# A Fourier layer in which a product, a norm's scaling and the reading of spectra are given other places in the order of work

## The chip, the cores and the metric

The kernel runs on one core of one Trainium2 chip. The core has five engines that the text names: TensorE (PE in the views, with PEld for its weight loads), VectorE (DVE), ScalarE (ACT), GpSimd (POOL) and SyncE (SP, which here only issues DMAs). Each engine works through its own instructions in the order in which the program lists them, and instructions wait on semaphores for work of other engines. The metric is the time of one execution of the whole program on the device, in microseconds (us), smaller is better.

## The reference, cut to what matters

Two inputs of 2048 and 512 positions by 1024 channels pass through two layers and a last norm. The first layer is windowed attention and isn't touched by the change. The second is Fourier mixing with a gate:

```python
def fourier_layer(x, g, w_gate, w_out):
    h = rmsnorm(x, g)
    hg = h.reshape(b, s, N_FGROUPS, FGROUP_CH)
    f = jnp.fft.fftn(hg, axes=(1, 3), norm="ortho").real
    gate = h @ w_gate
    return x + (f * jax.nn.silu(gate)) @ w_out
...
return rmsnorm(x, final_norm)
```

So each output row needs the transform over all positions (f), a product with the gate (silu of a projection), a projection back (w_out), the sum with the row of x, and a norm of that row with its scale.

## The kernel before, in words

The attention layer takes most of the span and is left out here. The Fourier layer transforms first over the channels and then over the positions. The positions are split by their remainder modulo 16: a short transform across the remainders gives spectra G[0] to G[8], and a 128 x 128 transform finishes each of them and gives 128 output rows (for k1 = 0 and 8) or two tiles of 128 rows (k1 and 16 - k1). The short input is treated likewise, with remainders modulo 4 (names with s0, s1, s2 instead of p0 to p8).

**A position.** `position(name, ...)` finishes one spectrum. Its loads are the gate's rows (`s2...`, 128 x 1024 each, from DRAM) and a table. For each half of the columns `halves_of` splits the spectrum into a high and a low part (`g..`, a cast on ACT, L1310, and a subtraction on DVE, L1311). PE multiplies them with the table into two PSUM banks (`A..`, `B..`); ACT copies A into `u..` (L1339, L1342), and DVE forms sums and differences with B (L1343 to L1346). At the end each tile u is multiplied by its gate's rows on DVE (L1348, 128 x 1024).

**A finish.** For the positions s0 to s2, p0, p8, p4 and p2, `split_T` transposes u on PE (`tru`) and splits it (`tTu`), and `finish(uT, r)` multiplies by the output weights. It loads 128 rows of x (`x2_r`, L1363), runs 24 matmuls of 512 columns into each of two PSUM tiles (`fo<r>_0`, `fo<r>_1`), adds them to x2 on DVE (L1374), and calls `normed`: a square with a sum on ACT (L969), the inverse root on DVE and POOL (`invf`, L88, L89), a scaling of 128 x 1024 on DVE (L1358) and the store by SP (L1359). `step` runs the positions of one spectrum, then finishes the tiles of the spectrum ahead of it.

**An Outs stage.** For p6, p1, p7, p3 and p5 the class `Outs` does the projection with fewer matmuls: `operands()` transposes the tiles (`tr6` and so on, 16 transposes on PE) and forms sums, differences and splits of them on ACT and DVE (`tT`, `F`, `S`; L1398, L1399, L1408, L1415, L942, L944), and `products` runs groups of 12 matmuls with weights and sums of weights (`Wo`, `Zo`, `Xo`; `fT`, `fN` are sums of weights that come back from DRAM, L1487), between which the hooks start the next position. `residual` and `normed` are the same as above (added by L1439).

**Rings.** The gate's rows and the x2 rows share one ring of four buffers of 128 x 1024 (tag "x"): a load into it waits until the tile that had the buffer is no longer needed. The PSUM tiles `fo`, `Wo`, `Zo`, `Xo`, and in the gates `W`, `Z`, `X`, share a ring of three banks (tag "acc"). The spectra G[7], G[3] and G[5] don't fit and go to DRAM (`god`, stored by ACT, L1637); `reads(k1)` brings each back as two tiles `go..` of 128 x 1024 (L1651).

**The gates.** `gates(pr, hooks)` makes the gate's rows of four tiles of positions with the same trick of shared products: groups of matmuls into W, Z and X, sums on DVE (the one of interest is `c22 += W`, L1142), then a tanh on ACT, a product on DVE (L1108) and a store. The hooks run other work between the groups; in the last call hook 3 holds the position s1 (`position(*one)`, tiles us1_0 and us1_1) and hook 5 its transposes.

The order of the instructions on each engine is settled when the program is built: a scheduler takes them from the code's order, moves independent ones past each other, and keeps what `after(ins, anchor)` asks for (ins is put behind anchor on the same engine, with no other effect).

Of the kernel before, what the change touches and what calls it, by code (L numbers as in the profile page):

```python
# [14 lines left out]
ALU = mybir.AluOpType  # L15
# [27 lines left out]
def encoder(  # L43
# [876 lines left out]
    def fourier_phase(tail):  # L920
        with ExitStack() as es:
# [15 lines left out]
            def zt(name):  # L937
                return right([P, D], F32, name)
# [134 lines left out]
                        ACT.activation(out, v[:, 1], AF.Copy, scale=scale)  # L1073
                        last_z[0] = DVE.scalar_tensor_tensor(out, v[:, 0], scale, out, ALU.mult, ALU.add)

            last_z = [None]

            def prod(out, a, b, ks, first):

# [14 lines left out]
            def gates(pr, hooks):  # L1094

                n, A, S = pr.n, pr.A, pr.S
                W = psum2.tile([P, 512], F32, tag="acc", name=f"W{n}")
                Z = psum2.tile([P, 512], F32, tag="acc", name=f"Z{n}")
                X = psum2.tile([P, 512], F32, tag="acc", name=f"X{n}")

                def x_step(k):
                    prod(X, A[0, 1], b21[4 * n : 4 * n + 4], (k,), True)
                    more()

                def silu(c, i, half):
                    th = main.tile([P, 512], F32, tag="xr", bufs=3, name=f"gt{pr.ts[i]}_{half}")
                    ACT.activation(th, c, AF.Tanh, scale=0.5)
                    DVE.scalar_tensor_tensor(th, th, 1.0, c, ALU.add, ALU.mult)  # L1108
                    t = pr.ts[i]
                    dst, t0 = (s2d[0], t) if t < SEQ // P else (s2d[1], t - SEQ // P)  # L1110
                    POOL.dma_start(dst[t0 * P : (t0 + 1) * P, half * 512 : half * 512 + 512], th)

                def hook(i):
                    for h in hooks.get(i, ()):
                        h()

                four = range(4)
                c = xtile([P, 2, 512], F32, f"c{n}")
                c11, c22 = c[:, 0], c[:, 1]
                prod(W, A[0, 0], wg["B11"], four, True)  # L1120
                ACT.copy(c11, W)
                hook(0)
                x_step(0)
                if pr is pairs[-1]:

                    more()
                    more()
                prod(Z, S[1], wg["T1"], four, True)
                ACT.copy(c22, Z)
                hook(1)  # L1130
                prod(W, S[2], wg["T2"], four, False)
                c12 = fp.tile([P, 512], F32, tag="c12", bufs=1, name=f"c12_{n}")
                ACT.copy(c12, W)
                hook(2)
                x_step(1)
                prod(Z, S[4], wg["B22"], four, False)
                DVE.tensor_tensor(c12, c12, Z, ALU.add)
                silu(c12, 0, 1)
                hook(3)
                x_step(2)  # L1140
                prod(W, S[3], wg["T3"], four, False)
                DVE.tensor_tensor(c22, c22, W, ALU.add)  # L1142
                silu(c22, 1, 1)
                hook(4)
                x_step(3)
                DVE.tensor_tensor(c11, c11, X, ALU.add)
                silu(c11, 0, 0)
                if pr is not pairs[-1]:
                    hook(5)
                prod(W, A[1, 1], wg["N4"], (0, 1), False)  # L1150
                if pr is pairs[-1]:
                    hook(5)
                prod(W, A[1, 1], wg["N4"], (2, 3), False)
                silu(W, 1, 0)
                hook(6)
# [156 lines left out]
                        out.append(t)  # L1312
                return out

            def position(name, tab, gr, gs, tiles, loads=None, parts=None, between=None):

                s2s, tb = loads or position_loads(name, tab, tiles)
                cs, sn, ns = [(tb[:, 2 * i], tb[:, 2 * i + 1]) for i in range(3)]
                bp = bank(f"B{name}")
                us = [zt(f"u{name}_{i}") for i in range(len(tiles))]  # L1320
                for hf in range(2):
                    ts = parts[hf] if parts else halves_of(name, gr, gs, hf)
                    if hf and between:
                        between()

                    def acc(out, tabs, c0, n):
                        for i, (w, t) in enumerate(zip(tabs, ts)):
                            v = [
                                t[:, part].rearrange("p (g c) -> p g c", g=2)[:, :, c0 : c0 + n]
                                for part in range(2)  # L1330
                            ]
                            matmul3(out, w, v, i == 0, i == len(ts) - 1)

                    a = bank(f"A{name}_{hf}")[:, :260].rearrange("p (g c) -> p g c", g=2)
                    acc(a, (cs, ns), 0, 130)
                    b = bp[:, hf * 256 : hf * 256 + 256].rearrange("p (g c) -> p g c", g=2)
                    acc(b, (sn, cs), P, P)
                    uv = [u.rearrange("p (g c) -> p g c", g=4)[:, 2 * hf : 2 * hf + 2] for u in us]
                    ACT.copy(uv[0][:, :, 0 : P + 1], a[:, :, 0 : P + 1])  # L1339
                    re, im = uv[0][:, :, 1:P], b[:, :, 1:P]  # L1340
                    for v in uv[1:]:
                        ACT.copy(v[:, :, 0 : P + 1 : P], a[:, :, 0 : P + 1 : P])  # L1342
                        DVE.tensor_tensor(v[:, :, 1:P], re, im, ALU.add)  # L1343
                        DVE.tensor_tensor(v[:, :, P + 1 : 256], re, im, ALU.subtract)
                    DVE.tensor_tensor(uv[0][:, :, P + 1 : 256], re, im, ALU.add)
                    DVE.tensor_tensor(re, re, im, ALU.subtract)  # L1346
                for u, s2 in zip(us, s2s):
                    DVE.tensor_tensor(u, u, s2, ALU.mult)  # L1348
                return list(zip(us, tiles))

            def out_rows(r):
                dst, off = (y_prompt, 0) if r[0] < SEQ else (y_sample, SEQ)
                return rows(dst, (r[0] - off, r[1]))

            def normed(x2, r):

                inv = sumsq(x2, f"f{r[0]}")
                DVE.scalar_tensor_tensor(x2, x2, inv[:, 0:1], gfb, ALU.mult, ALU.mult)  # L1358
                SP.dma_start(out_rows(r), x2)  # L1359

            def residual(r):
                x2 = x_tile(f"x2_{r[0]}")
# [3 lines left out]
            def finish(uT, r):  # L1366
                r0 = r[0]
                x2 = residual(r)
                for half in range(2):
                    ps = psum2.tile([P, 512], F32, tag="acc", name=f"fo{r0}_{half}")  # L1370
                    for k in range(KD):
                        matmul3(ps, uT[k], wo[half * KD + k], k == 0, k == KD - 1)
                    xs = x2[:, half * 512 : half * 512 + 512]
                    DVE.tensor_tensor(xs, xs, ps, ALU.add)  # L1374
                normed(x2, r)

# [138 lines left out]
                return name, 4 * k1, gl[0], gl[1] if len(gl) > 1 else None, tiles, (s2s, tb)  # L1517

            POOL.dma_start(mir, mirror)
            first, early, wo, w32f = [], [], [], []  # L1520

            def f_load(k):
                if k < 4:
# [18 lines left out]
            def turn_first(i):  # L1542
# [5 lines left out]
                0: [lambda: f_load(0)],  # L1548
                1: [lambda: f_load(1), lambda: early.append(sample(0, (0,), (left,), (xtile,), left))],
                2: [lambda: f_load(2), lambda: early.append(sample(2, (1,), (left,), (xtile,), left))],  # L1550
                3: [lambda: first.extend(position(*one)), lambda: f_load(3)],
                4: [lambda: f_load(4)],
                5: [lambda: turn_first(0), lambda: f_load(5)],
                6: [lambda: turn_first(1)],
            })
# [85 lines left out]
            finish(*pend.pop(0))  # L1641
            o.operands()
            finish(*pend.pop(0))
            o.load()

            def reads(k1):

                gl = []
                for i, src in enumerate(god[k1]):
                    g = zt(f"go{k1}_{i}")  # L1650
                    SP.dma_start(g, src)  # L1651
                    gl.append(g)
                return gl, table(f"p{k1}", k1, left)

            nxt = {"r": (G[1], table("p1", 1, left))}
            for k1, k2 in ((1, 7), (7, 3), (3, 5), (5, None)):
                name, tiles = f"p{k1}", pair(k1, 16, 0)
                gl, tb = nxt["r"]

                def split_g():  # L1660

                    nxt["s"] = [gated(name, r, place) for r, place in zip(tiles, (xtile, left))]
                    nxt["p"] = [halves_of(name, *gl, hf) for hf in range(2)]
                    if not ft["T3"]:
                        f_sums("T3", right)

                def transform(third):
                    if not ft["N4"]:
                        f_sums("N4", left)
                    nxt["o"] = Outs(k1, position(name, k1, None, None, tiles, (nxt["s"], tb), nxt["p"], third))  # L1670

                def turns():
                    nxt["o"].operands()
                    nxt["o"].load()
                    if k2:
                        nxt["r"] = reads(k2)

                o.products((split_g, transform, turns))
                o = nxt["o"]
# [102 lines left out]
```

## Time and profile before

| | before |
|---|---|
| time, median of 3 runs | 1588.15 us (1587.31 to 1588.84) |
| profiled execution | 1588.22 us |
| its span in the trace | 1586.5 us |
| mean granted clock of TensorE | 0.999 |
| busy: PE, PEld | 1573.1 us (99%), 1321.4 us (83%) |
| busy: DVE, ACT, POOL | 1153.0 (73%), 874.6 (55%), 445.6 us (28%) |
| DMA | 373.88 MB, mean 236 GB/s |

The span is the time from the first to the last event of the trace. 1.72 us of the profiled execution lie outside it. Busy is the time in which an engine has an instruction running; a wait of PE shows as the difference. Times in the timeline count from the span's start; the last gates call is at about 1310 to 1327 us, the finishes run from about 1326 to 1462 us, and the Outs stages from there to 1579 us.

### The profile page before, as it was taken

To read this page: it belongs to the slowest core of one execution; us is meant where nothing else is said; L and a number is where in the kernel's file an instruction comes from. 1 tells how busy PE (TensorE), PEld (TensorE's weight loads), DVE (VectorE), ACT (ScalarE), POOL (GpSimd) and SP (SyncE) were. 2 spreads that over 40 slices of the span, in tenths; PEclk is the share of its full clock that TensorE was granted. 3 is DMA by queue.
4 is the path that set the end of the run, shared out by engine and by line. 5 is a ranking of instruction groups with operands and counts; after the bars stand their busy time and mean duration, and the time that the engine had idled before them with its cause. 6 is when DMAs were issued, how large, how long until landed. Compare 5 with 4: busy or idle time off the path is not lost. (4 is left out here: it accounts for less than half of the span.)

```text
span 1586.5 us, 27419 instructions
## 1 busy us (share of the span) xinstructions
PE 1573.1 (99%) x9743; PEld 1321.4 (83%) x9743; DVE 1153.0 (73%) x2785; ACT 874.6 (55%) x2089; POOL 445.6 (28%) x613
## 2 busy tenths in 40 slices
PE   9999999999999999999999999999999999999998
PEld 7878888888888888988888888888888888888886
DVE  6788655887548786378764577669878878889796
ACT  6688534776246784167752476646555554343342
POOL 2466642421404314024222242223112111111010
PEclk9999999999999999999999999999999999999999
DMA  7588695565856567655649566665557469448752
GB/s 294 189 332 288 226 362 211 209 248 204 294 208 222 204 237 272 222 206 220 258 161 331 209 215 232 237 258 200 199 205 260 175 228 410 173 168 320 259 204 80
DMA packets 100580, 373.88 MB, mean 236 GB/s; under 512 B 12140, under 2 KB 22380, under 8 KB 83037
## 3 DMA queue, kind: packets, MB, share of 16 engines
q1 hardware_dynamic: 81708, 297.91, 52.4%
q0 software_dynamic: 16400, 70.04, 11.6%
q10 hardware_dynamic: 2336, 4.20, 0.7%
q8 instruction: 77, 1.26, 0.3%
q14 instruction: 59, 0.48, 0.1%
HBM read 280.84 MB, written 91.26 MB: 235 GB/s over the span
## 5 line engine op out<-in xcount | busy, mean ns | idle before, releaser
L489 DVE CUSTOM_DVE_ANT_0 S<-spt,b 128x385 f32<-128x385 f32 (+1 forms) x320 | 156.2, 527 | 114.5 <-PE spt L470 71.4
L95 PE MATMUL gp<-h,wg 128*128 128x512 f32 x960 | 237.6, 395 | 0.0
L95 PE MATMUL qp<-h,wq 128*128 128x512 f32 x960 | 237.3, 396 | 0.1
L95 PEld LDWEIGHTS qp<-h,wq 128*128 128x128 f32 x960 | 174.9, 188 | 37.3 <-DVE v L370 0.7
L95 PEld LDWEIGHTS gp<-h,wg 128*128 128x128 f32 x960 | 174.9, 188 | 37.1 <-issue 1.0
L497 ACT ACTIVATE S<-S 128x385 f32<-128x385 f32 (+1 forms) x320 | 188.8, 596 | 19.1 <-DVE S L489 18.6
L537 ACT CAST pts<-pt 128x384 fp32r<-128x384 f32 (+1 forms) x240 | 100.8, 461 | 176.6 <-PE pt L529 168.9
L538 DVE TENSOR_TENSOR pts<-pt,pts 128x384 fp32r<-128x384 f32 (+1 forms) x240 | 114.5, 523 | 18.9 <-ACT pts L537 18.8
L579 POOL TENSOR_TENSOR uT<-o,uT 128x256 fp32r<-128x256 f32 x75 | 55.4, 739 | 237.9 <-ACT uT L578 237.8
L95 PE MATMUL spt<-wo,uT 128*128 128x512 f32 x480 | 120.4, 391 | 0.0
L95 PE MATMUL op<-wo,uT 128*128 128x512 f32 x480 | 118.9, 391 | 0.0
L470 PE MATMUL spt<-kwin,qab 64*128 64x384 f32 (+1 forms) x960 | 118.6, 352 | 0.0
L555 PEld LDWEIGHTS av<-pts,v 128*128 128x128 f32 x576 | 101.3, 188 | 19.1 <-DVE pts L538 0.4
L555 PE MATMUL av<-pts,v 128*128 128x512 f32 (+1 forms) x576 | 115.9, 341 | 0.0
L95 PE MATMUL fo<-wo,tTu 128*128 128x512 f32 x480 | 115.3, 392 | 0.0
L95 PEld LDWEIGHTS op<-wo,uT 128*128 128x128 f32 x480 | 89.3, 188 | 18.6
L95 PEld LDWEIGHTS spt<-wo,uT 128*128 128x128 f32 x480 | 89.1, 188 | 18.4
L509 DVE TENSOR_SCALAR S<-S 128x384 f32<-128x384 f32 (+1 forms) x192 | 98.0, 511 | 6.8
L95 PEld LDWEIGHTS fo<-wo,tTu 128*128 128x128 f32 x480 | 88.3, 188 | 17.0
L470 PEld LDWEIGHTS spt<-kwin,qab 64*128 64x128 f32 x960 | 74.7, 186 | 28.4 <-issue 27.5
L575 POOL TENSOR_TENSOR o<-o,s 128x256 f32<-128x256 f32 x75 | 55.3, 737 | 132.0 <-DVE o L573 131.7
L529 PEld LDWEIGHTS pt<-ident,S 64*128 64x128 f32 x1344 | 79.0, 138 | 4.2 <-issue 1.9
(319 smaller groups left out, 3184.2 us busy)
## 6 DMA issues: line engine op xcount, KB each, us to landing
wo<-wsd SPq DMA_DIRECT2D x32, 1024.0 KB, 4.9
wq<-wsd SPq DMA_DIRECT2D x31, 1024.0 KB, 7.3
wg<-wsd SPq DMA_DIRECT2D x31, 1024.0 KB, 5.7
x<-x1d SPq DMA_DIRECT2D x40, 512.0 KB, 3.6
b<-b21d SPq DMA_DIRECT2D x40, 512.0 KB, 6.4
b<-rowd SPq DMA_DIRECT2D x40, 384.0 KB, 4.2
xs<-in_x_dram SPq DMA_DIRECT2D x23, 512.0 KB, 7.2
s2d<-gt POOLq DMA_DIRECT2D x40, 256.0 KB, 5.3
```

The source lines that it names most:

```text
L95: pe(PE.matmul(out, a[i], b[j], start=start and i + j == 0, stop=stop and i == 1, skip_group_check=more))
L470: pe(PE.matmul(banks[j][:, 2 + k0 * P : 2 + k1 * P], res["q"][rows, qp, b * P : (b + 1) * P], kwin[g][rows, kp, b * P + k0 * P : b * P + k ...
L489: seq(DVE, DVE.tensor_tensor_reduce(out=s[:, e0:e1], in0=ps[:, 1 + e0 : 1 + e1], in1=st["bias"][:, j, 386 - e1 : 386 - e0][:, ::-1], scale ...
L497: last_exp[0] = seq(ACT, ACT.activation(s[:, e0:e1], s[:, e0:e1], AF.Exp, bias=s[:, 386:387], scale=-1.0, accum_out=s[:, 387:388]))
L509: seq(DVE, DVE.tensor_scalar(s[:, ks], s[:, ks], den, None, ALU.mult))
L529: pe(PE.transpose(ps[h][:, kb, j, :], ss[j][rows, 1 + kb * P : 1 + (kb + 1) * P], ident[rows, rows]))
L537: seq(ACT, ACT.copy(hi, ps[:, k0:k1]))
L538: seq(DVE, DVE.tensor_tensor(lo, ps[:, k0:k1], f32(hi), ALU.subtract))
L555: pe(PE.matmul(to, v, pt, start=n == part == 0, stop=part == 1 and n in (1, len(todo) - 1), skip_group_check=n > 1,))
L575: eng.tensor_tensor(o, o, s, ALU.mult)
L579: low = eng.tensor_tensor(lo, o, f32(hi), ALU.subtract)
```

## The change

There are three edits, all in the Fourier layer. No instruction of an engine other than SP is added or taken away; SP issues six more DMAs.

1. **The gate's product of s1.** `position` takes a list `later`. With it, the two products u *= s2 of the position s1 (new line L1357) aren't issued at the position's end but from hook 4 of the last gates call, and each is put behind the sum `c22 += W` on DVE (`last_c`).
2. **The norm's scaling and store.** `normed` with `wait=True`, as `finish` calls it, does the square and the inverse root as before, but puts the scaling (new line L1370) and the store (L1371) on a list `due`. `scales()` empties it: at the end of the next `position`, behind its products in the code, with each scaling put behind the last subtraction of that position (`last_b`, new line L1352). After the last two finishes `scales()` is called once by hand, ahead of `o.load()` of stage p6. The Outs stages' own norms scale at once, as before.
3. **The spectra.** `reads` brings each `go` tile back in two DMAs of 128 x 512 instead of one of 128 x 1024, the first halves of both tiles first (new line L1669), and in the Outs stages the second half of a spectrum is split inside `position`, after the hook `between`, instead of ahead of it.

Lines of the new kernel that stand for old ones: L1349 to L1352 for L1343 to L1346, L1355 for L1348, L1379 for L1363, L1390 for L1374, L1407 for L1391, L1414 and L1415 for L1398 and L1399, L1424 and L1431 for L1408 and L1415 (a line number that stands in both kernels is another line in each), L1455 for L1439, L1503 for L1487.

```diff
-                DVE.tensor_tensor(c22, c22, W, ALU.add)
+                last_c[0] = DVE.tensor_tensor(c22, c22, W, ALU.add)
...
+            last_b, due = [None], []
+
+            def scales():
+                while due:
+                    due.pop(0)()
+
+            def position(name, tab, gr, gs, tiles, loads=None, parts=None, between=None, later=None):
...
                 for hf in range(2):
-                    ts = parts[hf] if parts else halves_of(name, gr, gs, hf)
                     if hf and between:
                         between()
+                    ts = parts[hf] if parts and parts[hf] else halves_of(name, gr, gs, hf)
...
-                    DVE.tensor_tensor(re, re, im, ALU.subtract)
+                    last_b[0] = DVE.tensor_tensor(re, re, im, ALU.subtract)
                 for u, s2 in zip(us, s2s):
-                    DVE.tensor_tensor(u, u, s2, ALU.mult)
+                    if later is None:
+                        DVE.tensor_tensor(u, u, s2, ALU.mult)
+                    else:
+                        later.append(lambda u=u, s2=s2: after(DVE.tensor_tensor(u, u, s2, ALU.mult), last_c[0]))
+                scales()
...
-            def normed(x2, r):
+            def normed(x2, r, wait=False):
                 inv = sumsq(x2, f"f{r[0]}")
-                DVE.scalar_tensor_tensor(x2, x2, inv[:, 0:1], gfb, ALU.mult, ALU.mult)
-                SP.dma_start(out_rows(r), x2)
+                def scale():
+                    after(DVE.scalar_tensor_tensor(x2, x2, inv[:, 0:1], gfb, ALU.mult, ALU.mult), last_b[0])
+                    SP.dma_start(out_rows(r), x2)
+                due.append(scale)
+                if not wait:
+                    scales()
...
-                normed(x2, r)
+                normed(x2, r, True)
...
-                3: [lambda: first.extend(position(*one)), lambda: f_load(3)],
-                4: [lambda: f_load(4)],
+                3: [lambda: first.extend(position(*one, later=products)), lambda: f_load(3)],
+                4: [lambda: [f() for f in products], lambda: f_load(4)],
...
             finish(*pend.pop(0))
             o.operands()
             finish(*pend.pop(0))
+            scales()
             o.load()
             def reads(k1):
-                gl = []
-                for i, src in enumerate(god[k1]):
-                    g = zt(f"go{k1}_{i}")
-                    SP.dma_start(g, src)
-                    gl.append(g)
+                gl = [zt(f"go{k1}_{i}") for i in range(2)]
+                for hf in range(2):
+                    cs = slice(hf * 512, hf * 512 + 512)
+                    for g, src in zip(gl, god[k1]):
+                        SP.dma_start(g[:, cs], src[:, cs])
                 return gl, table(f"p{k1}", k1, left)
...
-                    nxt["p"] = [halves_of(name, *gl, hf) for hf in range(2)]
+                    nxt["p"] = [halves_of(name, *gl, 0), None]
...
-                    nxt["o"] = Outs(k1, position(name, k1, None, None, tiles, (nxt["s"], tb), nxt["p"], third))
+                    nxt["o"] = Outs(k1, position(name, k1, *gl, tiles, (nxt["s"], tb), nxt["p"], third))
```

More of the change, by code (lines that the diff above doesn't have):

```diff
@@ L1074, in z_odd_even @@
                         last_z[0] = DVE.scalar_tensor_tensor(out, v[:, 0], scale, out, ALU.mult, ALU.add)
-            last_z = [None]
+            last_z, last_c = [None], [None]
             def prod(out, a, b, ks, first):
@@ L1313, in halves_of @@
                 return out
-            def position(name, tab, gr, gs, tiles, loads=None, parts=None, between=None):
+            last_b, due = [None], []
[3 more added lines that the diff above has]
+            def position(name, tab, gr, gs, tiles, loads=None, parts=None, between=None, later=None):
                 s2s, tb = loads or position_loads(name, tab, tiles)
@@ L1519, in fourier_phase @@
             POOL.dma_start(mir, mirror)
-            first, early, wo, w32f = [], [], [], []
+            first, early, wo, w32f, products = [], [], [], [], []
             def f_load(k):
```

## The prediction

> **What bounds the kernel now.** I read the page first for the span and the busy times, then PE's waits, then the timelines of PE, DVE and SP around each of them. The page's first part:
>
> ```profile
> span 1586.5 us, 27419 instructions
> ...
> PE 1573.1 (99%) x9743; PEld 1321.4 (83%) x9743; DVE 1153.0 (73%) x2785; ACT 874.6 (55%) x2089; POOL 445.6 (28%) x613
> ```
>
> PE is busy in all but 13.4 us of the span, so the work on PE sets the time, and an edit that leaves that work alone can only add or remove idle time of PE. PE's waits (total, times, longest):
>
> ```profile
> PE Ap L95 <- ACT gp L1310: 1.5, 1, 1.5
> PE idle L242 <- DVE idle L239: 1.2, 1, 1.2
> PE W L95 <- DVE c L1142: 1.0, 1, 1.0
> ...
> PE Bp L95 <- DVE up L1346: 0.3, 1, 0.3
> PE Ap L95 <- DVE gp L1311: 0.3, 1, 0.3
> PE Wo L95 <- DVE x L1439: 0.2, 1, 0.2
> ```
>
> The five that lie in the Fourier layer are all the change can take away: 3.2 us by the timeline below. About 0.2% of the time, 3.2 us, is also what a measurement of this kernel can tell from no change. The best case is thus only just visible, and the question is what new idle the new order makes. The sums are made against the profiled execution, 1588.22 us, 0.07 us above the median of the runs.
>
> PE's timeline, start, length, operation, count, and in brackets idle time before it:
>
> ```profile
> 1.18 5.30 PE L242 MATMUL idle<-idle 128*128 128x512 bf16 x12 [1.18 <-DVE idle L239]
> ...
> 1322.00 1.65 PE L95 MATMUL W<-wN,tTb 128*128 128x512 f32 x6 [1.01 <-DVE c L1142]
> ...
> 1412.93 0.74 PE L95 MATMUL Bp<-gp,tbp 128*128 128x256 f32 x4 [0.26 <-DVE up L1346]
> ...
> 1444.49 0.63 PE L95 MATMUL Ap<-gp,tbp 128*128 128x260 f32 x3 [0.26 <-DVE gp L1311]
> ...
> 1449.75 0.88 PE L95 MATMUL Bp<-gp,tbp 128*128 128x256 f32 x6
> 1450.47 5.63 PE L95 MATMUL fo<-wo,tTu 128*128 128x512 f32 x24
> 1455.94 1.91 PE L1391 MATMUL tr<-ident,up 128*128 128x128 f32 x16
> 1457.61 4.34 PE L95 MATMUL fo<-wo,tTu 128*128 128x512 f32 x18
> 1461.78 2.88 PE L95 MATMUL Wo<-wo,tT 128*128 128x512 f32 x12
> 1464.50 2.88 PE L95 MATMUL Zo<-fT,S 128*128 128x512 f32 x12
> ...
> 1484.52 3.04 PE L95 MATMUL Wo<-fN,tT 128*128 128x512 f32 x12 [0.19 <-DVE x L1439]
> ...
> 1494.22 0.39 PE L95 MATMUL Ap<-gp,tbp 128*128 128x260 f32 x1 [1.51 <-ACT gp L1310]
> ```
>
> From start to start, 12 matmuls of 512 columns take 2.72 us (1461.78 to 1464.50), 0.227 each, 24 take 5.47, and 16 transposes 1.67.
>
> **The gate's product.** DVE's timeline around the wait of 1.01 us:
>
> ```profile
> 1319.79 1.22 DVE L1348 TENSOR_TENSOR us<-us,s2s 128x1024 f32<-128x1024 f32 x1
> 1320.93 0.41 DVE L1346 TENSOR_TENSOR us<-us,Bs 128x254 f32<-128x254 f32 x1
> 1321.26 0.68 DVE L1142 TENSOR_TENSOR c<-c,W 128x512 f32<-128x512 f32 x1
> 1321.86 1.22 DVE L1348 TENSOR_TENSOR us<-us,s2s 128x1024 f32<-128x1024 f32 x1
> ```
>
> The sum on which PE waits (L1142) stands behind the first product, 1.14 us from start to start. In the changed order it stands ahead of both, so it ends up to 1.14 us earlier and the wait of 1.01 goes. Behind it the product of us1_0, the gate's L1108 and the product of us1_1 follow. The transposes that need the two products come after six and after twelve more matmuls of W (1.4 and 3.6 us with the first transposes), against product ends at about 1.1 and 2.9 us behind the sum: covered, with 0.3 to 0.7 to spare; if that cover failed it would cost up to 0.4. Gain 1.0, bounds 0.6 and 1.0.
>
> **The norm's scaling ahead of p6.** The two waits of 0.26 stand behind such a scaling on DVE (1.2 us), which now comes later: gain 0.5, bounds 0.3 and 0.5. With that PE reaches stage p6 about 1.5 us earlier, and I keep before's times below, since only distances count.
>
> **What the scaling does in p6.** This is the part that decides. DVE's timeline there:
>
> ```profile
> 1451.66 1.22 DVE L1348 TENSOR_TENSOR up<-up,s2p 128x1024 f32<-128x1024 f32 x1
> 1452.80 0.41 DVE L1346 TENSOR_TENSOR up<-up,Bp 128x254 f32<-128x254 f32 x1
> 1453.13 1.28 DVE L1358 SCALAR_TENSOR_TENSOR x<-x,invf,gfb 128x1024 f32<-128x1024 f32 x1
> 1454.32 1.22 DVE L1348 TENSOR_TENSOR up<-up,s2p 128x1024 f32<-128x1024 f32 x1
> ...
> 1457.19 0.69 DVE L1399 TENSOR_TENSOR tT<-tr,tT 128x512 fp32r<-128x512 f32 x1 [1.06 <-ACT tT L1398]
> ...
> 1463.38 0.68 DVE L1399 TENSOR_TENSOR tT<-tr,tT 128x512 fp32r<-128x512 f32 x1
> 1463.98 0.67 DVE L1374 TENSOR_TENSOR x<-x,fo 128x512 f32<-128x512 f32 x1
> ```
>
> Before, the sums of fo2_0 and fo2_1 into x2_2 were done before the transposes, so the three banks of the ring were free, and fo14_1's 24 matmuls ran around the transposes: 6 ahead of them and 18 behind (1457.61). Those 18 cover the time in which ACT and DVE turn the transposes into operands: 11 operations on DVE, 1457.19 to 1463.98.
>
> The scalings of x2_4 and x2_12 now wait for the end of position p6. Until then each holds a buffer of the ring of four; p6's two gate tiles hold the other two. So the load of x2_2 can't be issued before the first product is done, and SP takes it up still later, behind the store of x2_12 and three loads of fT2. The scheduler, for which x2_2 is late, lists the sum of fo2_0 behind all 11 operand operations and one split of the next spectrum (L1311). In the changed order PE has: the last 20 matmuls of fo14_0, the 16 transposes, 8 of the 12 matmuls of p1's first A and B, then all 24 of fo14_1. The first of these needs fo2_0's bank, and so that sum. Nothing else of PE stands between. So fo14_1 no longer covers the operands, it waits for them.
>
> Step by step. (a) At the transposes: DVE's chain from the end of B (1449.75 + 0.74 = 1450.49) to the end of the second product (1454.32 + 1.14 = 1455.46) has one scaling between the products in both orders, 4.97 us; PE's cover is 20 matmuls, 4.56, where it was 24. New wait 0.4, and 0.1 for the release: 0.5. (b) From the transposes' start (1455.94) to the first operation of DVE 1.25 us; 11 operations 6.79; the split and the sum 0.60 each; release 0.1: 9.3. PE does in it 16 transposes and 8 small matmuls (0.88 for 6 is the listed length, 0.72 from start to start, so 0.12 each): 1.67 + 0.96 = 2.6. Idle 6.7. In the new order four operations that write F stand in a row ahead of the splits S, so DVE may also wait once for ACT's copy, 0.6 or so by the length of one operation. I take 7.0, bounds 6.0 and 7.4. The instructions counted here are the same as before, only their cover is gone, so a bound below 6 would need DVE faster than in this trace.
>
> (c) x2_2 must have landed by then. The transposes start with the second product; then the scaling of x2_12 (1.2), its store, three loads, and x2_2's issue.
>
> ```profile
> 1447.03 2.95 SPq L1487 DMA_DIRECT2D fT<-fT2d x4
> ```
>
> ```profile
> x<-x1d SPq DMA_DIRECT2D x40, 512.0 KB, 3.6
> ```
>
> ```profile
> DMA packets 3627, 13.11 MB, mean 375 GB/s; under 512 B 400, under 2 KB 400, under 8 KB 3624
> ...
> x<-x1d SPq DMA_DIRECT2D x4, 512.0 KB, 10.2
> ```
>
> The first row gives 0.74 an issue, so x2_2 is issued about 1.2 + 0.4 + 3 x 0.74 = 3.8 us after the transposes' start and needed at 8.6: 4.8 to land. The median over the program is 3.6 (second row, of the page), in the busy window 1440 to 1475 it was 10.2 (third view). Store, three loads and x2_2 are 2.6 MB, 7.0 us at that window's 375 GB/s, from about 1.3 on: 8.3. So it is just in time; I add nothing, and 0 to 5.4 (3.8 + 10.2 - 8.6) is the bound.
>
> **The clock of TensorE.** The chain of waits shows what follows the gap of 1.51 us (the first of its rows here is used in the next part):
>
> ```profile
> 1483.61 9.86 DMA go<-god
> ...
> 1494.85 1.82 PE Wo L95 x8
> ```
>
> There PE ran on at once at full speed, 8 matmuls in 1.82 us. At the program's start, after 1.2 us in the trace and an unknown time before it, 12 matmuls of 512 columns took 5.30, 0.44 each, against 0.227. So PE starts at half speed when it has been idle long, and loses 12 x (0.44 - 0.227) = 2.5 us. A gap of 7 us has no row; bounds 0 and 2.5, and since it is far longer than the one that cost nothing, I take 2.5. [...]
>
> **The spectra in halves.** Ap7 waited 1.51 for the reading of go7, whose loads took 9.86 to land. In the changed order go7 is issued ahead of the store of x2_6 and only the first half of each tile is needed for the first split, while PE has 48 matmuls between the transposes tr1 and Ap7, 10.9 us (39 before, 8.9). Even with all of 9.86 it comes in time: gain 1.5, bounds 0 and 1.5. The second halves are split after the third group, some 3 us before PE takes them. The six added DMA issues lie on SP, which idles. The 0.19 before `fN` goes as PE is later by then.
>
> **Sum.** -1.0 - 0.5 + 0.5 + 7.0 - 1.5 - 0.2 = +4.3, and 2.5 for the clock: +6.8. 1588.2 + 6.8 = **1595.0 us**, slower by 0.43%. Behind p7 PE has no idle time that could give any of it back, as the stretch from there to PE's end shows (its limits and length, then PE's busy time):
>
> ```profile
> 1496.00:1579.00 83.00, 83.00 (x418) 69.83 (x417) 65.87 (x112) 29.67 (x63) 9.75 (x11) 1.00 0.40 139
> ```
>
> **Rivals.** (1) The clock doesn't fall: the same without 2.5, 1592.5. For it: the 1.51 gap. Chance 0.22, against 0.45 for the forecast. (2) x2_2 lands late, in the state of the busy window: up to 5.4 more, 1600.4; half of it 1597.7. For it the 10.2, against it that the fT1 loads are issued earlier now. 0.15. [...] 0.10. (4) Not slower: fo14_1 isn't held up, because the bank that it takes is one whose sum DVE has done by then, and not fo2_0's. Then the five waits go and 0.5 comes: 1588.2 - 2.7 = 1585.5. It decides if PE's idle time at fo14_1 is under 2.7. For it that three banks are in turn and fo14_1 is the fourth tile, so the case hangs on one sum alone; against it the listed order, in which that sum is the fo2_0 one. 0.08, of which 0.01 goes to "same". That an edit does nothing is possible for go7 alone, and costs the 1.5 that is in the bounds.
>
> **How the numbers follow.** Slower by over 0.2%: 0.45 + 0.22 + 0.15 + a part of (3), 0.02 = 0.84; same: 0.08 of (3) and 0.01 of (4) = 0.09; faster 0.07. The range leaves out (4) and most of (3), 0.16, and the top of (2), 0.04: from 1590.5 (rival 1 with the low bound of the idle time, 1591.5, and 1 us into rival 3) to 1600 (rival 2).
>
> **What would show it.** Right: in the changed profile a wait of PE of 6 to 8 us, `fo` on the sum of x and fo (L1390), just behind the transposes of p6 at about 1455 to 1463; no wait of W at 1321; matmuls of 0.44 each behind the gap. The DVE row of the sum stands behind the last `S`. Wrong: fo runs on behind the transposes; or the gap is there and the matmuls behind it take 0.227 (rival 1); or the gap ends with the landing of x2_2 and not with DVE's row ahead of it (rival 2).

## The result, and the profile after

| | before | after |
|---|---|---|
| time, median of 6 runs each | 1588.97 us (1587.31 to 1591.3) | 1596.3 us (1595.38 to 1597.83) |
| ratio of after to before | | 1.0046, 95% interval 1.0035 to 1.0057 |
| profiled execution, its span | 1588.22, 1586.5 us | 1597.73, 1595.6 us |
| PE busy | 1573.1 us | 1575.9 us |
| mean granted clock | 0.999 | 0.993 |

The change made the kernel 7.3 us slower, 0.46%. Between the two profiled executions there are 9.1 us: PE was idle 19.7 us where it had been 13.4, and took 2.8 us longer for the same 9743 matmuls. 1.3 us of the idle time lie in the program's first 20 us (`spt`, 1.9 us where before had 0.6), which the change does not touch, and in this execution the granted clock was at half from 7.5 to 10.9 us. Together they make PE 1.85 us later by the last gates call (1322.84, and the wait of 1.01 that is gone, against 1322.00). So 7.25 of the 9.1 us are left for the change; the profiled execution was one of the slower ones of the changed kernel.

PE's waits after the change (total, times, longest):

```profile
PE Ap L95 <- ACT gp L1310: 7.1, 2, 6.4
PE spt L95 <- ACT h L220: 1.9, 1, 1.9
...
PE tr L1407 <- DVE up L1355: 0.6, 1, 0.6
PE Ap L95 <- DVE gp L1311: 0.5, 1, 0.5
```

The five waits of the Fourier layer of before are gone from the list. In their place stand four that all lie at one spot (the first row has the name of before's longest wait, but that one was at p7, and these are the first matmuls of p1, behind p6's transposes). PE's timeline, first at the gates, then at p6:

```profile
1322.84 1.66 PE L95 MATMUL W<-wN,tTb 128*128 128x512 f32 x6
...
1448.66 4.72 PE L95 MATMUL fo<-wo,tTu 128*128 128x512 f32 x20
1453.95 1.94 PE L1407 MATMUL tr<-ident,up 128*128 128x128 f32 x16 [0.57 <-DVE up L1355]
1462.29 0.58 PE L95 MATMUL Ap<-gp,tbp 128*128 128x260 f32 x1 [6.40 <-ACT gp L1310]
...
1463.57 0.80 PE L95 MATMUL Ap<-gp,tbp 128*128 128x260 f32 x2 [0.49 <-DVE gp L1311]
...
1465.51 0.58 PE L95 MATMUL Ap<-gp,tbp 128*128 128x260 f32 x1 [0.71 <-ACT gp L1310]
...
1466.28 8.34 PE L95 MATMUL fo<-wo,tTu 128*128 128x512 f32 x24
1474.46 2.88 PE L95 MATMUL Wo<-wo,tT 128*128 128x512 f32 x12
```

Before, 18 matmuls of fo14_1 ran on right behind the 16 transposes. Now PE stands 6.4 us after them, does eight small matmuls with gaps, and all 24 of fo14_1 begin at 1466.28. They take 8.18 us to the next group where 24 took 5.47, and the small ones are slow too (the first takes 0.38 us to the next, where the prediction's rows give 0.12). Two things held fo14_1. One is the sum of fo2_0, which frees its bank. DVE's timeline shows it (the sums of fo2_0 and fo2_1 are the row of L1390):

```profile
1455.28 0.69 DVE L1415 TENSOR_TENSOR tT<-tr,tT 128x512 fp32r<-128x512 f32 x1 [0.28 <-ACT tT L1414]
...
1459.22 0.69 DVE L944 TENSOR_TENSOR S<-F,S 128x512 fp32r<-128x512 f32 x1 [0.74 <-ACT S L942]
...
1461.63 1.28 DVE L944 TENSOR_TENSOR S<-F,S 128x512 fp32r<-128x512 f32 x2
1462.84 0.68 DVE L1311 TENSOR_TENSOR gp<-g1r,gp 128x512 fp32r<-128x512 f32 x1
1465.54 1.28 DVE L1390 TENSOR_TENSOR x<-x,fo 128x512 f32<-128x512 f32 x2 [2.02 <-DMA x<-x1d]
```

All eleven operand operations come first, then the split, then 2.02 us in which DVE waits for the rows x2_2 to land, then the sum. The other is PE's own order: the eight small matmuls stand ahead of fo14_1, and they need splits of the next spectrum, whose casts stand behind the operands on ACT and whose subtraction (L1311) stands behind them on DVE. ACT's rows, and PE's weight load for fo14_1:

```profile
1461.61 0.62 ACT L1310 CAST gp<-g1r 128x512 fp32r<-128x512 f32 x1
1464.84 0.62 ACT L1310 CAST gp<-g1s 128x512 fp32r<-128x512 f32 x1 [2.60 <-PE Bp L95]
```

```profile
1466.28 3.92 PEld L95 LDWEIGHTS fo<-wo,tTu 128*128 128x128 f32 x10 [0.28 <-DVE x L1390]
```

The two end almost together: when the small matmuls were through, the weight load waited for the sum another 0.28 us. SP's timeline shows how late these rows were asked for: behind the stores of the two deferred tiles and three loads of fT2.

```profile
1452.70 2.67 SPq L1371 DMA_DIRECT2D out_dram<-x  x2
1455.42 2.33 SPq L1503 DMA_DIRECT2D fT<-fT2d  x3
1457.85 2.20 SPq L1379 DMA_DIRECT2D x<-x1d  x4
```

The first product of p6, which gives back a buffer of the ring, had ended at about 1451.1; the load was issued at 1457.85.

The windows over PE give the granted clock (limits, length, PE busy and count, clock, DMA share, GB/s):

```profile
1457.00:1458.00 1.00, 0.00 (x0) 1.00 0.56 156
1458.00:1459.00 1.00, 0.00 (x0) 0.58 1.14 385
...
1468.00:1470.00 2.00, 2.00 (x6) 0.50 0.51 203
...
1471.00:1472.00 1.00, 1.00 (x4) 0.60 0.94 385
1472.00:1474.00 2.00, 2.00 (x10) 1.00 1.02 313
```

The clock falls from 1.00 to 0.50 some 2.3 us after PE's last transpose (1455.89) and is back at 1.00 at about 1471.8, 5.5 us after fo14_1 began to run without a gap.

### The profile page after: what moved, and what is told of

It reads as the page before. It is cut to its first block, busy times and chain, and to the rows that moved or that the text cites. A ratio compares the mean times of both kernels' runs of the same rounds, so it can differ in the third digit from the quotient of the medians.

```text
span 1595.6 us, 27439 instructions
## 1 busy us (share of the span) xinstructions
PE 1575.9 (99%) x9743; PEld 1325.4 (83%) x9743; DVE 1153.1 (72%) x2785; ACT 874.9 (55%) x2089; POOL 451.9 (28%) x613
## 5 line engine op out<-in xcount | busy, mean ns | idle before, releaser
L95 PEld LDWEIGHTS fo<-wo,tTu 128*128 128x128 f32 x480 | 90.4, 192 | 18.1 <-DVE x L1390 0.3
```

The costliest lines, as they stand in the source:

```text
L95: pe(PE.matmul(out, a[i], b[j], start=start and i + j == 0, stop=stop and i == 1, skip_group_check=more))
```

## The experiments

Theory A: the place of x2_2's load in SP's order and of its sum in VectorE's order makes the stall at p6, and the fallen clock adds to it; the other two edits gain. Rival B: the ring, in which the deferred tiles hold the buffers that x2_2 needs. Rival C: the landing of x2_2 alone. A fourth view is that the loss has its cause in the other two edits.

**The deferred scaling alone (e1)** (the product at the position's end, whole reads, as before):

```diff
-                3: [lambda: first.extend(position(*one, later=products)), lambda: f_load(3)],
-                4: [lambda: [f() for f in products], lambda: f_load(4)],
+                3: [lambda: first.extend(position(*one)), lambda: f_load(3)],
+                4: [lambda: f_load(4)],
...
-                    nxt["p"] = [halves_of(name, *gl, 0), None]
+                    nxt["p"] = [halves_of(name, *gl, hf) for hf in range(2)]
...
```

> The deferred scaling and store of the norm alone, with the gate's product and the reading of the spectra as before. Theory A (the deferral makes the stall at p6, the other two edits only gain): the whole loss is here, 1597 to 1598.5 us against 1589 before, a wait of PE of 6 to 7 us behind the transposes of p6 and matmuls of 0.34 us behind it, and the wait of W of 1.0 us is back. Rival (the loss comes from the six added DMAs or from the moved product): 1588.5, no stall at p6.

Measured: 1597.3 us, ratio 1.0052 (1.0038 to 1.0066). PE's timeline has the same stall:

```profile
1463.30 0.59 PE L95 MATMUL Ap<-gp,tbp 128*128 128x260 f32 x1 [6.40 <-ACT gp L1310]
```

The 24 matmuls of fo14_1 take 8.20 us, and the wait of W of 1.0 us is back. The stall, and all of the changed kernel's loss, come with this edit alone. The wait for go7 at p7 is gone here too, though the spectra are read whole.

**The two waiting scalings ahead of p6 (e2).**

```diff
+            scales()
             o = Outs(6, position("p6", 6, *G[6], pair(6, 16, 0)))
```

> The changed kernel, with the two waiting scalings (x2_4, x2_12) issued ahead of position p6, so that their buffers of the ring come free some 10 us earlier. In the order of SP the load of x2_2 still stands behind all eight loads of fT, and in that of VectorE the sum of fo2_0 still behind the eleven operand operations. Theory A (the place of the load and of the sum in these orders makes the stall): PE still idles 6 to 7 us there, 1593 to 1596 us. Rival B (the ring makes it: the scalings hold the buffers that x2_2 needs): the stall goes, 1585 to 1587 us.

Measured: 1595.77 us, ratio 1.0044 (1.003 to 1.0057). PE's timeline there:

```profile
1459.78 0.58 PE L95 MATMUL Ap<-gp,tbp 128*128 128x260 f32 x1 [5.03 <-ACT gp L1310]
...
1464.32 7.92 PE L95 MATMUL fo<-wo,tTu 128*128 128x512 f32 x24 [1.98 <-DVE x L1390]
```

The buffers came free early, and PE still idled 5.0 + 0.7 + 2.0 us and took 7.75 us for the 24 matmuls. Rival B falls: a free ring does not help while the load and the sum keep their places in the two orders. The loads of x2 rows were issued from 1450.51 on, behind the eight loads of fT, and DVE still waited 2.30 us for the first to land, until 1463.57.

**The loads of fT2 behind the finishes (e3).**

```diff
             f_sums("T1", right)
-            f_sums("T2", right)
             finish(*pend.pop(0))
             o.operands()
             finish(*pend.pop(0))
             scales()
+            f_sums("T2", right)
             o.load()
```

> The changed kernel with one line moved: the four loads of fT2 are written behind the finishes of p2, not ahead of them. The scalings wait as in the changed kernel, and hold the ring as long. In the order of SP the load of x2_2 now stands ahead of the two stores and of fT2, and in that of VectorE the sums of fo2_0 and fo2_1 stand right behind the first operand operation. Theory A: fo14_1 starts about 1 us behind the transposes, 1586 to 1588 us, matmuls at 0.227 us. Rival B (the ring): x2_2 is still issued only behind the product, so 1592 us or more. Rival C (the landing of x2_2 alone): the stall shrinks only by the 2.0 us that VectorE waited for the landing, 1594 us.

Measured: 1594.14 us, ratio 1.0037 (1.0023 to 1.0051). The time is not the one that A gave, so the timelines have to say why. PE's:

```profile
1453.22 1.94 PE L1407 MATMUL tr<-ident,up 128*128 128x128 f32 x16 [0.57 <-DVE up L1355]
1455.89 5.74 PE L95 MATMUL fo<-wo,tTu 128*128 128x512 f32 x24 [0.73 <-DVE x L1390]
...
1487.13 2.83 PE L1407 MATMUL tr<-ident,up 128*128 128x128 f32 x16 [4.37 <-DVE up L1355]
1489.61 3.83 PE L95 MATMUL Wo<-fN,tT 128*128 128x512 f32 x12
```

DVE's:

```profile
1454.55 0.69 DVE L1415 TENSOR_TENSOR tT<-tr,tT 128x512 fp32r<-128x512 f32 x1 [0.28 <-ACT tT L1414]
1455.16 1.28 DVE L1390 TENSOR_TENSOR x<-x,fo 128x512 f32<-128x512 f32 x2
```

SP's:

```profile
1450.45 0.32 SPq L1379 DMA_DIRECT2D x<-x1d  x1
```

At p6 the timelines are as A said: the two sums stand behind the first operand operation, fo14_1 starts 0.73 us late, and its 24 matmuls run at full speed (5.58 us to the next group, granted clock 1.00) and end at 1461.47, ahead of before's 1461.78. B and C had this stall stay or shrink by 2 us. The load is issued just behind the first product, so the ring still sets its earliest time, and that is early enough. Three orders differ from the changed kernel's here: SP's, DVE's, and PE's as well, in which the small matmuls of p1 no longer stand ahead of fo14_1. No run moves one of them alone, so their shares are not shown. What ate the gain is a new stall one stage later: this order puts the second B of p1 three matmuls ahead of the transposes of p1, which then wait 4.37 us for the subtractions, the products and a scaling on DVE between them, and the clock falls again (0.50 from 1489 to 1491, 12 matmuls in 3.67). The forecast of 1586 to 1588 looked at one stage, and missed the order that the scheduler found for the next.

**Filling the gap (e4).**

```diff
+                    ab = bank(f"A{name}_{hf}")
+                    if name == "p1" and not hf:
+                        for _ in range(30):
+                            after(PE.matmul(ab, wo[0][0][:, :P], wo[0][0], start=True, stop=True), last_t[0])
...
```

> The changed kernel with 30 extra matmuls of 512 columns, without use, into the bank of A of p1 behind the transposes of p6, so that PE works through most of the gap (30 x 0.227 = 6.8 us). The order elsewhere is that of the changed kernel, but for one more split (0.6 us) ahead of the sum of fo2_0. If the gap lowers PE's clock, the 24 matmuls of fo14_1 take 5.5 us instead of 8.2, and the 8 to 12 small ones 1.5 instead of 2.6, and the time falls by 2 to 3 us to 1593.5 to 1594.5. If the slow matmuls have another cause (the weights, a busy memory), they stay slow and the time stays at 1596.3 to 1597.

Measured: 1594.15 us, ratio 1.0036 (1.0022 to 1.005). PE's timeline:

```profile
1455.11 7.11 PE L1343 MATMUL Ap<-wo 128*128 128x512 f32 x30
...
1465.82 5.73 PE L95 MATMUL fo<-wo,tTu 128*128 128x512 f32 x24
```

With 30 useless matmuls more the median is 2.2 us lower (1596.3 in the changed kernel); as ratios to the kernel before, measured beside each, it is 0.10% lower, and the two intervals overlap, so the time alone would not show it. The trace does: the granted clock is 1.00 from 1455 to 1472, and fo14_1 takes 5.57 us from start to start. It starts 12.40 us behind the transposes' start, as late as in the changed kernel (12.33), though the small matmuls run at full speed here (the first takes 0.12 us to the next). The slow matmuls were the clock's doing, and the clock was the gap's.

**The norms of the two finishes behind position p2 at once, the rest deferred (e5).**

```diff
-                normed(x2, r, True)
+                normed(x2, r, r0 not in (4, 12))
...
+            scales()
             o = Outs(6, position("p6", 6, *G[6], pair(6, 16, 0)))
```

> The changed kernel, but the scalings of x2_4 and x2_12, the two that p6 would hold back, are issued at once as before; all other deferred scalings, the moved product and the halves stay. The order at p6 is again the one of before: both sums of fo2 ahead of the transposes, fo14_1 around them (10 matmuls ahead, 14 behind). Theory A: no stall at p6, and the gains are left: 1.0 (W), 0.3 (Bp of p2), up to 1.5 (go7) off 1588.5: 1585.5 to 1587 us. Rival (the other deferred scalings cost too, or the gains are not there): 1588 us or more.

Measured: 1592.68 us, ratio 1.0026 (1.0016 to 1.0035). The stall behind the transposes is gone, as A said, but the time is 4 us above before. One cause stands in PE's timeline, with DVE's row for it:

```profile
1444.94 0.63 PE L95 MATMUL Ap<-gp,tbp 128*128 128x260 f32 x3 [1.69 <-DVE gp L1311]
```

```profile
1444.20 0.69 DVE L1311 TENSOR_TENSOR gp<-ev,gp 128x512 fp32r<-128x512 f32 x1
```

Before had this split at 1443.75 and a wait of 0.26. Here it comes 0.45 later, while PE arrives 1.0 earlier for the moved product: 0.26 + 0.45 + 0.98 = 1.69. Why it comes later is not shown. DVE has little room there, but it is not fuller than before (busy 37.99 us of the 40 from 1400 to 1440, before 38.65); its longest idle time is 1.59 us ahead of the scaling at 1426.93 (before 0.16), for an inverse root that POOL does behind the issue of a gather of gate rows. In the changed kernel that scaling had left the stretch, and DVE does not wait there. A second part lies at p7, 0.9 + 0.9 + 0.6 us for the halves of go7, about which e8 says more; the rest of the 4 us is not settled.

**Product and halves, no deferral (e6).**

```diff
-                scales()
                 return list(zip(us, tiles))
...
-                    after(DVE.scalar_tensor_tensor(x2, x2, inv[:, 0:1], gfb, ALU.mult, ALU.mult), last_b[0])
+                    DVE.scalar_tensor_tensor(x2, x2, inv[:, 0:1], gfb, ALU.mult, ALU.mult)
...
-                normed(x2, r, True)
+                normed(x2, r)
```

> The moved product and the halves together, every norm scaled at once as before. Theory A: 1588.5 - 1.0 - 1.5 = 1586.0, between 1585.5 and 1587. Against e5 it tells what the deferred scalings ahead of p2 are worth by themselves: 0.3 by the wait that they took away.

Measured: 1590.28 us, ratio 1.0009 (1.000 to 1.0018). No stall at p6, the wait of W is gone, but PE waits 1.9 us at Ap of p7 where before waited 1.5. One of the two gains isn't there; the next two experiments take the edits apart.

**The product alone (e7).**

```diff
-                    DVE.tensor_tensor(u, u, s2, ALU.mult)
+                    if later is None:
+                        DVE.tensor_tensor(u, u, s2, ALU.mult)
+                    else:
+                        later.append(lambda u=u, s2=s2: after(DVE.tensor_tensor(u, u, s2, ALU.mult), last_c[0]))
...
```

> The moved product alone. The wait of W of 1.0 us goes: 1587.5. Rival (the transposes or the next step wait for the products instead): 1588.5, with a new wait of PE between 1322 and 1340.

Measured: 1587.77 us, ratio 0.9992 (0.9983 to 1.0001). The wait of W is gone and no wait of PE stands between 1322 and 1340. But the wait for go7 at p7, where nothing was changed, is another one too:

```profile
1493.36 0.39 PE L95 MATMUL Ap<-gp,tbp 128*128 128x260 f32 x1 [0.20 <-ACT gp L1310]
```

Before had 1.51 there. With the spectra read whole, this wait varied from one profiled execution to the next (0.67 us in e10).

**The halves alone (e8).**

```diff
+                gl = [zt(f"go{k1}_{i}") for i in range(2)]
+                for hf in range(2):
+                    cs = slice(hf * 512, hf * 512 + 512)
+                    for g, src in zip(gl, god[k1]):
+                        SP.dma_start(g[:, cs], src[:, cs])
...
```

> The halves alone. If the first halves of go7 land 1.5 us or more ahead of the old landing, the wait of 1.51 goes: 1587.0. Rival (the time to landing does not depend on the size: the load is issued at the same place, and the queue ahead of it sets when it lands): the wait stays, 1588.5.

Measured: 1590.33 us, ratio 1.0013 (1.0004 to 1.0022): neither the gain nor no change, but slower by 1.6. ACT's and DVE's rows at p7, with PE's wait:

```profile
1492.07 1.19 ACT L1310 CAST gp<-go 128x512 fp32r<-128x512 f32 x2 [2.09 <-DMA go<-god]
```

```profile
1491.51 0.69 DVE L1311 TENSOR_TENSOR gp<-go,gp 128x512 fp32r<-128x512 f32 x1
1494.34 0.15 DVE L88 TENSOR_SCALAR invf<-ssf 128x1 f32<-128x1 f32 x1 [2.14 <-ACT jkf L969]
1494.41 0.68 DVE L1311 TENSOR_TENSOR gp<-go,gp 128x512 fp32r<-128x512 f32 x1
```

```profile
1495.15 0.51 PE L95 MATMUL Ap<-gp,tbp 128*128 128x260 f32 x2 [1.70 <-DVE gp L1311]
```

The cast that waited for the half starts at 1492.07, and in before at 1493.55; but with whole reads it starts at 1492.70 in e7 and at 1492.49 in e10, so that the half lands much earlier is not shown. On DVE its split stands behind the small operation of the norm of x2_10, which waits for a square that ACT does behind the casts. DVE idles 2.14 us ahead of it, most of that with the split ready to run. This profile is of the fastest of the eleven executions (1588.83), and its wait at p7 is only 0.2 us longer than before's; where the rest of the 1.6 lies is not shown.

**The split ahead of that operation (e9)** (with the product and the halves of e6):

```diff
...
+                    inv = last_i[0]
                     nxt["p"] = [halves_of(name, *gl, 0), None]
+                    if name == "p7":
+                        after(inv, last_s[0])
```

> Product and halves as in e6, and on VectorE the small operation of the norm of x2_10 (invf, L88 of before) is put behind the first two splits of go7, where e6 and e8 had it between them. In e8 that operation waited 2.1 us for a square on ScalarE, and the second split, for which TensorE waited 1.7 to 1.9 us, stood behind it. If that order is what gave back the gain of the halves, the wait at Ap of p7 falls to 0.5 us or less and the time to 1587 to 1588.7 us, against 1590.3 for e6. If the halves cost by their six more DMAs or by the landing, the wait stays over 1.3 us and the time at 1590.

Measured: 1588.1 us, ratio 0.9998 (0.9989 to 1.0007). DVE's rows:

```profile
1492.25 0.69 DVE L1313 TENSOR_TENSOR gp<-go,gp 128x512 fp32r<-128x512 f32 x1 [1.31 <-ACT gp L1312]
1493.83 0.15 DVE L88 TENSOR_SCALAR invf<-ssf 128x1 f32<-128x1 f32 x1 [0.88 <-ACT jkf L971]
```

The split starts 0.65 us behind the start of its cast, in e8 2.34 us, and the waits at Ap of p7 are 0.4 and 0.2 us (1.9 in e6). The order of two instructions on DVE had made that wait, and the six more DMAs cost nothing that shows here. A gain of the halves does not show either: the product alone, measured beside this run, has 1587.5 us.

**The product alone once more (e10).**

> The moved product alone once more, on the chip and beside the runs of e9, since it is the only one so far that came out below the kernel before: 1587.8 us against 1588.7 (0.9992, 0.9983 to 1.0001). The gain of 1.0 that theory A gives it would show as 0.9994; chance would show as 1.000.

Measured: 1587.5 us, ratio 0.9996 (0.9987 to 1.0005). In the two comparisons the medians are 0.9 us below before, the size of the wait that it takes away, and each interval still holds 1. It has the lowest medians of all versions; that it beats the kernel before is not shown. For it speaks the wait of W, gone from both profiles. The spans (1585.7 and 1585.5 us against 1586.5) say little, since the wait at p7, which this edit does not touch, is 0.20 and 0.67 us in them and 1.51 in before.

## Why the prediction was right, point by point

The forecast was 1595.0 us, between 1590.5 and 1600.0, with the stall at p6 as its cause; measured were 1596.3. The place, the cause and the size are right; how near the sum came is in part luck, as the last point shows.

- *The product, 1.0 gained*: the wait is gone in every kernel with this edit. The edit alone had medians 0.9 lower twice, with 1 inside both intervals.
- *The two waits of 0.26*: gone. Whether the deferral costs anything else ahead of p6 was not asked. In e5, where the scalings of x2_4 and x2_12 are back at their old place, PE waits 1.69 us there; why is not shown.
- *(a), 0.5 at the transposes*: 0.57. The release, taken as 0.1, is 0.14 there, from the end of the second product on DVE (1452.59 + 1.22) to the transposes (1453.95).
- *(b), idle 7.0*: 6.40 + 0.49 + 0.71 = 7.6. DVE's first operation came 1.33 us behind the transposes' start (1.25 forecast), the eleven took 7.56 (6.79 and one wait of 0.6 for ACT's copy; that wait was 0.74). What the step had wrong are the eight small matmuls, which it took as cover of 0.96 us. They covered nothing: they needed splits made behind the same operands, ran at the end of the gap, in pieces and at half clock, and held fo14_1 as long as the sum did. So the wait does not stand at `fo` on the sum, as the sign on record had it, but at `Ap` on ACT's cast, and from the transposes' start to fo14_1 it took 12.3 us and not 9.3. The orders as the cause are shown by e3, which took this stall away, and by e2, which freed the ring and did not; that DVE's order alone would have made it is argued.
- *(c), x2_2 just in time*: too early by 2.0. Its issue came 3.9 us behind the transposes' start (3.8 forecast), but it landed 11.6 behind it and not 8.3. Its reading was 2.6 MB at the 375 GB/s of before's window, from 1.3 us on; the window from 1455.28 to the landing has 323 GB/s over 10.26 us, 3.3 MB. So both were off, and what the other 0.7 MB were is open. The price was small: PE's weight load for fo14_1 waited 0.28 us for the sum, since the small matmuls ran until 1466.3 anyhow.
- *The clock, 2.5*: 24 matmuls in 8.18 for 5.47 are 2.7. e4, with the clock at 1.00, has 5.57 for them. PE's busy time rose by 2.8, but that number mixes in the small matmuls and the program's start. The row of the program's start, from which the 2.5 was read, does not show a lowered clock: the windows have a granted clock of 1.00 from 1.18 to 6.50 us both in before, where the 12 matmuls took 5.30 us, and in the changed kernel, where they took 4.17. So the 2.5 does not follow from that row. What the runs show in its place is the clock behind the gap: it went from 1.00 to 0.50 2.3 us after the last transpose and back to 1.00 5.5 us after unbroken work began.
- *The halves, 1.5 gained*: the wait did go in the changed kernel, but not by the halves: it is gone in e1 as well, which reads the spectra whole. PE had 48 matmuls between the transposes and Ap7, which the prediction counted and which suffice alone. And the 1.5 was one sample of a wait that varies: 0.20 in e7 and 0.67 in e10, with whole reads. In the order without the deferral the medians with halves are 1.6 us (e8) and 2.5 us (e6 against e7) higher, and with the split ahead (e9) no gain shows.
- *The sum, +6.8*: 7.3 between the medians. From the transposes' start to p6's first group the changed kernel takes 20.5 us and the one before 5.8. Six matmuls of fo14_1 and eight small ones lie in it that lay outside before, 2.3 us at the prediction's prices; so 12.3 us were lost there, and the sum has 9.5 (7.0 and 2.5). The other stretches, beyond the gains in the sum and without the program's start, came out 2.4 us shorter, which the sum does not have: the 96 small matmuls of the positions between the gates and p6 take 16.8 us for 18.1 (16.4 in e1), and the rest is open. That these two errors nearly cancel is luck.

Rival 1 (the clock stays up) is refuted by the granted clock of 0.50 and by e4. Rival 2 (late landing) came in part, 2.0 of its 5.4, with almost no price. No run shows what rival 3 needed, a shorter gap with the clock up: DVE did not close up (the eleven operations took 7.56 us, one wait of 0.74 among them), PE's gaps were 7.6 us together, and behind e3's gap of 4.37 us the clock was 0.50. Rival 4 needed fo14_1 to be freed by another sum than that of fo2_0; it was not.

## What to carry to other kernels

Before an operation is put off, look at what its tile holds, what is listed behind it on each queue, and who waits for those: here a scaling of 1.2 us that nobody needed at once held up a load, the load's sum was sorted behind eleven other operations, and a PSUM bank waited for the sum. Look also at what stands ahead on the waiting engine: here eight small matmuls, listed first, needed the same operands. One group of matmuls had covered the making of the next group's operands here, and when it was no longer free to run, the stage lost that cover (7.6 us idle), not the length of the moved operation (1.28). And the stalls of TensorE of 4.4 to 6.4 us here were paid twice, once as idle time and once in the slower matmuls behind them (24 in 8.18 us for 5.47 in the changed kernel, 12 in 3.67 for 2.72 in e3); the wait of 1.5 us in before was not (8 matmuls in 1.82, granted clock 1.00). A wait that one profile shows may be another in the next execution (1.51, 0.20 and 0.67 us at p7), so look at several before counting on it.

## What the runs showed of the hardware

In these runs the clock did not follow the gap at once. After PE's last matmul it stayed at 1.00 for about 2.3 us in the changed kernel and 4.0 us in e2; in e3, with a gap of 4.37 us from 1482.8 on, it fell only when PE was already at work again:

```profile
1487.00:1488.00 1.00, 0.87 (x8) 1.00 0.93 334
1488.00:1489.00 1.00, 1.00 (x7) 0.51 1.11 180
...
1491.00:1492.00 1.00, 1.00 (x5) 0.79 0.97 383
```

So in e3 the work just behind the gap still ran at 1.00 and that from 1488.0 on at 0.50, some 5 us after PE stopped. The clock was low for 3.4 us there and for 13.65 us in the changed kernel, 4 of them before PE took up work and 4 more in which that work had gaps itself.

Short windows over each change of the clock in the changed kernel's trace, at the program's start and at p6, give its moment, as an estimate: the clock is 1.00 on one side of each and 0.50 on the other, and a window with a change in it shows a mean of the two:

```profile
7.40:7.60 0.20, 0.20 (x2) 0.72 1.12 440
10.80:11.00 0.20, 0.20 (x2) 0.75 1.11 430
1458.00:1458.20 0.20, 0.00 (x0) 0.88 1.02 410
1471.80:1472.00 0.20, 0.20 (x2) 0.99 1.02 410
```

By these means it falls at 7.49, rises at 10.90, falls at 1458.15 and rises at 1471.80, and is low for 3.41 and for 13.65 us. In e2 the means of 0.86 from 1458 to 1459 and of 0.76 from 1468 to 1470 put the low time at about 10.2 us. What sets these moments and lengths is not shown. The gap ahead of the first of these falls was 1.85 us, from 5.36 to 7.21; in before the gap at that place was 0.57 us, and the clock there is 1.00.
